# PEER row gathers spread over the second stage, and DeltaNet head norms begun at the scans' ends, in a one-core diffusion layer

## Chip, cores and metric

One core of one Trainium2 chip runs the whole layer in one launch. The metric is device time in microseconds; lower is better. The times of the kernel before are three runs: 2075.72, 2077.7 and 2087.32 us, median 2077.7 us.

## What is computed

A layer over 512 latent tokens (D = 1024) with 256 context tokens ahead of them, then a final norm; all in fp32. Cut to what matters here:

```python
m = project_mixer_inputs(h, w_in, ...)            # q, k, v of attention and DeltaNet, z, gates
o_attn = windowed_attention(...)
o_dn, _, _ = bidirectional_delta(m, ..., st_f, st_b)   # 4 heads of 128, scans in both directions
o_dn = gated_head_norm(o_dn, m['z_dn'], dn_norm)  # o * rsqrt(mean(o*o, -1) + eps) * gain * silu(z), per token and head
x = x + gt1 * (m['gate_attn'] * (o_attn @ w_br_attn) + m['gate_dn'] * (o_dn @ w_br_dn)) @ w_out
h2 = rmsnorm(x, norm_ffn) * (1.0 + sc2) + sh2
x = x + gt2 * peer_ffn(h2, ...)                   # 8 heads x top 16 of 128*128 experts for each token:
                                                  # sum of gate * gelu(h2 . u_table[e]) * v_table[e]
return rmsnorm(x, final_norm)
```

## The kernel before

TensorE multiplies in pairs of high and low halves: each fp32 operand is split into a rounded high part (a cast on ScalarE) and the rest (a subtraction on GpSimd or VectorE), and `mm3` (lines 173 to 176) issues three products for each.

**DeltaNet** (up to 632 us). `dn_front`, `dn_batch` and `dn_scan(h)` are generators that a loop (lines 1032 to 1053) steps in turn, at a raised priority; the build's scheduler then orders the instructions of each engine by priority and by when it reckons them ready. The scans of the four heads overlap in part. `dn_scan` makes six steps; a step's state update goes TensorE, ScalarE (`vt`, line 936, a tile with two buffers that all scans share), TensorE, VectorE. From the third step on it writes the token outputs `od[:, l, h]` (lines 963 to 966), each from both directions.

**Merge** (lines 1202 to 1253). All sixteen pairs of token block `l` and head `h` get a square with a sum on ScalarE (line 1206), into `oss`; one scaling, one square root, one reciprocal and one multiplication of all of `od` follow (lines 1208 to 1211). Then head by head: a gate tile is loaded (`gate_tile`, line 1199, three buffers), TensorE transposes the head (1216), VectorE multiplies by gate and gain (1217), and ScalarE and VectorE split the result into `dT` (1218, 1219). The products with w_br_dn follow (lines 1238 to 1253). The rows gt1b, sh2b, a2b and the norm's gain are loaded after that in the program (1257 to 1261), and VectorE scales gt1b and makes a2b (1260, 1262). `out_proj` (line 1274) multiplies by w_out in eight chunks for a pair of token blocks and then uses gt1b (1295) and a2b (1303).

**PEER** takes two ways. For three of the four token blocks (ND = 3) all 128 blocks of 128 experts are computed densely: `first_product` multiplies u by the tokens, a gelu follows, then the weighting by a gate matrix (from DRAM, `gg`) and `second_product` with v, accumulated in PSUM. In the first stage `nb` = 112 blocks get their first product, and the activations go to DRAM (`Ad`); the second stage computes the other 16, and makes the second product of all 128. The fourth token block (LG) gathers: each of 128 (head, choice) rows of u, then of v, is read for all 128 tokens by one indirect DMA on GpSimd's queue into one of four `grow` buffers (lines 1439, 1450); VectorE makes a dot product of each u row (1432) and adds each v row to `accg` (1454).

The gathers run as a side task, `gu = Side(chain(gather_u(), gather_v()))`: `run(us)` adds credit, and the generator goes on as long as credit is left; a row costs 1.2 (0.3 for the first three). GpSimd's and VectorE's order is the program's own here. In the second stage's loop, slot `n` computes block `ORDER[n]` (the 16 new ones first), prepares the operands of block `n - 5` (`operands`, lines 1533 to 1553: loads of v, gates and stored activations on the SP queue, weighting on VectorE, casts on ScalarE), gives the gathers credit, and issues the second product of the block before. In the credit, `first` is true for slots 5 to 15:

```python
            first, put_by = b >= nb and n < NBLK, ORDER[n - SKEW] < nb
            gu.run(GF * (4.18 - 1.25 - 1.1 + (4.16 - 2.5) * first))
            if not fin and (gu.done or n == NBLK + SKEW - LAST - 1):
                gu.run(1e9)
                finish(LG)
```

`finish(LG)` (lines 1574 to 1601) adds the residual and applies the final norm for the gathered block. `second_product` subtracts for the low halves (1556, 1557) and holds the last four blocks (LAST = 4) back, to run them as one group by token block. The three dense blocks are finished after it.

Of the kernel before, what the change touches and what calls it, by code (L numbers as in the profile page):

```python
# [62 lines left out]
MWAIT = 3  # L63
SKEW = 5
OT = 4
GF = 1.0
GWAIT = 2
TKG = 3.6
GU = 0.8
# [67 lines left out]
def body(ctx: ExitStack, tc: tile.TileContext, I, out, dbg=lambda *a: None):  # L137
# [5 lines left out]
    def const(shape, name, dt=F32):  # L143
        return cp.tile(shape, dt, name=name, tag=name)
# [768 lines left out]

    scanned = set()

    def dn_scan(h):

        unit = heads[h]["unit"]
# [2 lines left out]
        for step in range(6):  # L921
# [48 lines left out]
                dbg(f"S{h}", Sn)  # L970
            yield
        scanned.add((h, 6))

# [52 lines left out]
    live, scans, nscan = [], [], 0  # L1028
    side = [beside()]
    tick = 0  # L1030
    oss = const([P, NLB, 4], "oss")
    while front or live or batches or scans or nscan < 4:
        with tc.high_priority(offset=FIRST):
            with tc.high_priority(offset=FRONT):
# [165 lines left out]
        return t  # L1200


    for l in range(NLB):
        for h in range(4):
            junk = gst([P, P], "junkn", bufs=2)
            S.activation(junk, od[:, l, h], AF.Square, accum_out=oss[:, l, h:h + 1])
    dbg("od", od)
    V.tensor_scalar(oss, oss, 1.0 / P, EPS, op0=ALU.mult, op1=ALU.add)
    S.activation(oss, oss, AF.Sqrt)
    V.reciprocal(oss, oss)  # L1210
    V.tensor_tensor(od, od, oss[:, :, :, None].to_broadcast([P, NLB, 4, P]), op=ALU.mult)
    for h in range(4):
        szh = gate_tile(16 + h)
        pt = psum()
# [42 lines left out]
    SP.dma_start(gt1b, bc(arows[0], P, D))  # L1257
    SP.dma_start(sh2b, bc(arows[1], P, D))
    SP.dma_start(a2b, bc(arows[2], P, D))
    V.tensor_scalar(gt1b, gt1b, 0.5, None, op0=ALU.mult)  # L1260
    SP.dma_start(nfb, bc(I["norm_ffn"][0], P, D))
    V.scalar_tensor_tensor(a2b, a2b, 1.0, nfb, op0=ALU.add, op1=ALU.mult)

    qp = mg.tile([P, HEADS, SEQ], F32, name="qp", tag="dT")
    h2T_hi = mp.tile([P, KC, SEQ], F32R, name="h2T_hi", tag="oT")
# [8 lines left out]
    def out_proj(pair):  # L1274
# [5 lines left out]
        for k in range(KC):  # L1280
            raw = raw_tile()
            SP.dma_start(raw, I["w_out"][0, k * P:(k + 1) * P])
            hi, lo = split(raw)
            for l in pair:
                ls = slice(l * P, (l + 1) * P)
                for j in range(2):
                    js = slice(j * 512, (j + 1) * 512)
                    mm3(acc[l, j], yT_hi[:, k, ls], yT_lo[:, k, ls], hi[:, js], lo[:, js], k == 0, k == KC - 1)
# [110 lines left out]
    def gate_matrices(l):  # L1399
# [5 lines left out]
        for t0 in range(0, P, TB):  # L1405
# [21 lines left out]
            for i0 in range(0, KEYS, 32):  # L1427
                S.dma_start(Gd[pc, :, i0:i0 + 32], stg[:, i0:i0 + 32])

    def gather_u():  # L1430
        def dot(j, u):
            V.tensor_tensor_reduce(out=u, in0=u, in1=h2p if stage[0] < 2 else h2g, scale=1.0, scalar=0.0, op0=ALU.mult, op1=ALU.add,  # L1432
                                   accum_out=act[:, j:j + 1])
            return 1.2

        held = []
        for j in range(P):
            u = gp.tile([P, D], F32, name="grow", tag="grow", bufs=4)
            G.indirect_dma_start(out=u, out_offset=None, in_=UT_, in_offset=bass.IndirectOffsetOnAxis(ap=exi[:, j:j + 1], axis=0))  # L1439
            held.append((j, u))  # L1440
            yield dot(*held.pop(0)) if len(held) > DOTLAG else 0.3
        for x in held:
            yield dot(*x)
        S.activation(act, act, AF.Gelu_apprx_tanh)
        V.tensor_tensor(act, act, gateg, op=ALU.mult)

    def gather_v():
        for j in range(P):
# [3 lines left out]
                V.tensor_scalar(accg, v, act[:, 0:1], None, op0=ALU.mult)  # L1452
            else:
                V.scalar_tensor_tensor(accg, v, act[:, j:j + 1], accg, op0=ALU.mult, op1=ALU.add)  # L1454
            yield 1.2

    def transpose_u(b):

# [144 lines left out]
    for n in range(NBLK + SKEW):  # L1603
# [12 lines left out]
                ws[n] = w  # L1616
        if n >= SKEW:
            nxt.append(operands(n - SKEW, ws.pop(n - SKEW, None)))
            first, put_by = b >= nb and n < NBLK, ORDER[n - SKEW] < nb
            gu.run(GF * (4.18 - 1.25 - 1.1 + (4.16 - 2.5) * first))  # L1620
            if not fin and (gu.done or n == NBLK + SKEW - LAST - 1):
                gu.run(1e9)
                finish(LG)
            if len(nxt) > 1:
                second_product(*nxt.pop(0))
# [43 lines left out]
```

## Time and profile before

| | before |
|---|---|
| median of 3 runs | 2077.7 us (2075.72 to 2087.32) |
| profiled execution, its own time | 2080.87 us |
| its span | 2079.1 us |
| mean granted TensorE clock | 0.969 |
| TensorE (PE) | 1928.9 us busy, 93% |
| VectorE (DVE) | 1643.1 us, 79% |
| ScalarE (ACT) | 951.1 us, 46% |
| GpSimd (POOL) | 976.9 us, 47% |
| HBM traffic | 228 GB/s over the span |

The profiled execution is one run on its own; its time is 3.2 us above the median. Busy shares are averages over all stages. A busy TensorE is pipelined, and the ends of its matmuls are modelled. The row "idle before" or the bracket behind an instruction names what ended the idle time of its engine.

### The profile page before, as it was taken

The numbers are of one execution on the slowest core, as the hardware profiler recorded it, in microseconds if no ns is written. First come the engines' busy times: TensorE is split into PE (matmuls) and PEld (weight loads), VectorE is DVE, ScalarE is ACT, GpSimd is POOL, SyncE is SP. The second block draws the span as 40 slices with busy tenths as digits, with TensorE's granted clock in tenths as the row PEclk, the third lists the DMA queues.
The fourth block names the chain that finished last, engine by engine and source line by source line (L and its number), as shares of the span: only waits on it lengthen the run. The fifth ranks groups of instructions, "written<-read, shape, count | busy, mean of one in ns | idle before, by whom it ended". The sixth has DMA issues, their size and how long they took to land.

```text
span 2079.1 us, 29606 instructions
## 1 busy us (share of the span) xinstructions
PE 1928.9 (93%) x10018; PEld 1627.8 (78%) x10018; DVE 1643.1 (79%) x3304; ACT 951.1 (46%) x1769; POOL 976.9 (47%) x695
## 2 busy tenths in 40 slices
PE   6999999999897897999999999899889999999998
PEld 2766666788786696989999999888778777777786
DVE  4599885378776768799998999666879898989855
ACT  5545544333333443333766666895323333333333
POOL 2655534311212872677565666443445555555200
PEclk9999999999998998999999999999999999999999
DMA  9333322422515685889889878789999999999963
GB/s 308 92 112 116 107 82 81 127 84 63 138 51 182 201 195 158 234 234 252 242 255 266 246 236 256 242 259 309 300 315 376 386 386 393 389 391 397 352 233 107
DMA packets 283477, 475.87 MB, mean 229 GB/s; under 512 B 35224, under 2 KB 197293, under 8 KB 282813
## 3 DMA queue, kind: packets, MB, share of 16 engines
q1 hardware_dynamic: 214251, 277.82, 43.9%
q0 software_dynamic: 36864, 134.23, 18.9%
q10 hardware_dynamic: 32210, 61.93, 8.4%
q8 instruction: 79, 1.29, 0.3%
q14 instruction: 73, 0.60, 0.1%
HBM read 409.71 MB, written 64.18 MB: 228 GB/s over the span
## 4 chain that ended last, share of the span: by engine, by line
PE 36%; DMA 17%; DVE 14%; issue 14%; POOL 12%; ACT 5%; ACTq 1%; SPq 1%; DVEq 0%; POOLq 0%
DMA grow<-in_peer_v_dram,exi 7%; POOL w_lo L1470 7%; POOL grow L1439 3%; PE pg L176 3%; PE pg L175 3%; PE pg L174 3%; PE pacc L175 3%; PE pacc L176 2%; PE pacc L174 2%; PE pa L176 2%; PE pa L174 2%; PE pa L175 2%; DMA rep<-ad 2%; DVE accg L1454 2%; PE pm L1422 2%
## 5 line engine op out<-in xcount | busy, mean ns | idle before, releaser
L1470 POOL TENSOR_TENSOR w_lo<-ut,w_hi 128x512 fp32r<-128x512 f32 x224 | 293.9, 1335 | 231.4 <-ACT w_hi L1466 225.3
L174 PE MATMUL pa<-h2T_hi,w_hi 128*128 128x384 f32 x1024 | 354.6, 346 | 35.2 <-ACT w_hi L1466 32.4
L176 PE MATMUL pa<-h2T_hi,w_lo 128*128 128x384 f32 x1024 | 361.2, 354 | 9.3 <-POOL w_lo L1470 8.4
L175 PE MATMUL pa<-h2T_lo,w_hi 128*128 128x384 f32 x1024 | 349.9, 342 | 0.0
L170 POOL TENSOR_TENSOR w_lo<-w_raw,w_hi 128x1024 fp32r<-128x1024 f32 x78 | 200.1, 2576 | 305.1 <-ACT w_hi L169 229.3
L1450 POOL DMA_INDIRECT grow<-in_peer_v_dram,exi x128 | 200.0, 1563 | 168.0 <-DVE accg L1454 143.4
L1552 ACT CAST w_hi<-w_raw 128x1024 fp32r<-128x1024 f32 x124 | 130.3, 1051 | 226.3 <-DMA w_raw<-in_peer_v_dram 110.8
L175 PE MATMUL pacc<-w_lo,wh 128*128 128x512 f32 x744 | 214.0, 403 | 20.1 <-DVE w_lo L1556 19.5
L174 PEld LDWEIGHTS pa<-h2T_hi,w_hi 128*128 128x128 f32 x1024 | 198.3, 194 | 43.3 <-ACT w_hi L1466 42.8
L176 PEld LDWEIGHTS pa<-h2T_hi,w_lo 128*128 128x128 f32 x1024 | 197.8, 193 | 16.0 <-POOL w_lo L1470 13.1
L176 PE MATMUL pacc<-w_hi,wl 128*128 128x512 f32 x744 | 208.8, 396 | 0.0
L174 PE MATMUL pacc<-w_hi,wh 128*128 128x512 f32 x744 | 208.3, 395 | 0.0
L175 PEld LDWEIGHTS pa<-h2T_lo,w_hi 128*128 128x128 f32 x1024 | 197.5, 193 | 0.3
L1439 POOL DMA_INDIRECT grow<-in_peer_u_dram,exi x128 | 148.3, 1159 | 100.4 <-DVE act L1432 80.4
L175 PEld LDWEIGHTS pacc<-w_lo,wh 128*128 128x128 f32 x744 | 138.6, 190 | 63.0 <-DVE w_lo L1556 31.7
L1466 ACT CAST w_hi<-ut 128x1024 fp32r<-128x1024 f32 x126 | 132.6, 1053 | 114.6 <-DVE ut L1465 80.4
L1454 DVE SCALAR_TENSOR_TENSOR accg<-grow,act,accg 128x1024 f32<-128x1024 f32 x127 | 162.8, 1282 | 25.1 <-DMA grow<-in_peer_v_dram,exi 24.1
L1556 DVE TENSOR_TENSOR w_lo<-w_raw,w_hi 128x1024 fp32r<-128x1024 f32 x124 | 151.3, 1220 | 33.7 <-ACT w_hi L1552 33.7
L176 PEld LDWEIGHTS pacc<-w_hi,wl 128*128 128x128 f32 x744 | 140.6, 189 | 34.3
L174 PEld LDWEIGHTS pacc<-w_hi,wh 128*128 128x128 f32 x744 | 139.4, 188 | 34.7 <-ACT wh L1543 0.5
L1465 DVE STREAM_TRANSPOSE ut<-w_raw 128x1024 f32<-128x1024 f32 x126 | 155.8, 1238 | 10.7 <-DMA w_raw<-in_peer_u_dram 7.9
L174 PE MATMUL pg<-hL_hi,w_hi 128*128 128x512 f32 (+1 forms) x336 | 139.6, 416 | 0.0
(447 smaller groups left out, 4115.9 us busy)
## 6 DMA issues: line engine op xcount, KB each, us to landing
w_raw<-in_peer_u_dram SPq DMA_DIRECT2D x512, 128.0 KB
w_raw<-in_peer_v_dram SPq DMA_DIRECT2D x128, 512.0 KB
Gd<-stg ACTq DMA_DIRECT2D x48, 512.0 KB
gg<-Gd SPq DMA_DIRECT2D x16, 1536.0 KB
Ad<-ga ACTq DMA_DIRECT2D x112, 192.0 KB
aa<-Ad SPq DMA_DIRECT2D x28, 768.0 KB
w_raw<-in_w_ada_dram SPq DMA_DIRECT2D x40, 512.0 KB
w_raw<-in_w_in_dram SPq DMA_DIRECT2D x34, 512.0 KB
```

Source lines behind the costliest of these rows:

```text
L170: (lo_eng or G).tensor_tensor(lo, raw, hi.bitcast(F32), op=ALU.subtract)
L174: PE.matmul(o, lh, rh, start=start, stop=False)
L175: PE.matmul(o, lh, rl, start=False, stop=False)
L176: PE.matmul(o, ll, rh, start=False, stop=stop)
L1439: G.indirect_dma_start(out=u, out_offset=None, in_=UT_, in_offset=bass.IndirectOffsetOnAxis(ap=exi[:, j:j + 1], axis=0))
L1450: G.indirect_dma_start(out=v, out_offset=None, in_=VT_, in_offset=bass.IndirectOffsetOnAxis(ap=exi[:, j:j + 1], axis=0))
L1454: V.scalar_tensor_tensor(accg, v, act[:, j:j + 1], accg, op0=ALU.mult, op1=ALU.add)
L1465: V.transpose(lf.rearrange("p (c f q) -> p c f q", f=4, q=32), u.rearrange("p f (c x) -> p c f x", x=32))
L1466: S.copy(hi, lf)
L1470: eng.tensor_tensor(lo[:, cs], lf[:, cs], hi[:, cs].bitcast(F32), op=ALU.subtract)
L1552: S.copy(vh, v)
L1556: V.tensor_tensor(vl, v, vh.bitcast(F32), op=ALU.subtract)
```

## The change

At the end of the scans of heads 0, 1 and 2 the squares of the head's four token blocks and the scaling of their sums are issued (`head_norm`); `oss` is laid out by head and made before the scans. In the merge the three heads get square root, reciprocal and a multiplication of their own each, then head 3 its squares and the rest. The two VectorE instructions on gt1b and a2b are issued in `out_proj`, at the fifth chunk of w_out of the first pair. In PEER's second stage the credit of a slot is the rows still to do, times 1.3, shared over the slots up to 127, where a slot that computes a new block counts twice; a v row costs 1.3 instead of 1.2.

```diff
+    oss = const([P, 4, NLB], "oss")
+    def head_norm(h):
+        junk = dn.tile([P, 2, P], F32, name="vt", tag="vt", bufs=2)
+        for l in range(NLB):
+            S.activation(junk[:, l % 2], od[:, l, h], AF.Square, accum_out=oss[:, h, l:l + 1])
+        V.tensor_scalar(oss[:, h], oss[:, h], 1.0 / P, EPS, op0=ALU.mult, op1=ALU.add)
...
         scanned.add((h, 6))
+        if h < 3:
+            head_norm(h)
...
+    def scale_heads(hs):
+        S.activation(oss[:, hs], oss[:, hs], AF.Sqrt)
+        V.reciprocal(oss[:, hs], oss[:, hs])
+        for h in range(4)[hs]:
+            V.tensor_tensor(od[:, :, h], od[:, :, h], oss[:, h, :, None].to_broadcast([P, NLB, P]), op=ALU.mult)
+    scale_heads(slice(0, 3))
     for l in range(NLB):
-        for h in range(4):
-            junk = gst([P, P], "junkn", bufs=2)
-            S.activation(junk, od[:, l, h], AF.Square, accum_out=oss[:, l, h:h + 1])
-    V.tensor_scalar(oss, oss, 1.0 / P, EPS, op0=ALU.mult, op1=ALU.add)
-    S.activation(oss, oss, AF.Sqrt)
-    V.reciprocal(oss, oss)
-    V.tensor_tensor(od, od, oss[:, :, :, None].to_broadcast([P, NLB, 4, P]), op=ALU.mult)
+        junk = gst([P, P], "junkn", bufs=2)
+        S.activation(junk, od[:, l, 3], AF.Square, accum_out=oss[:, 3, l:l + 1])
+    V.tensor_scalar(oss[:, 3], oss[:, 3], 1.0 / P, EPS, op0=ALU.mult, op1=ALU.add)
+    scale_heads(slice(3, 4))
...
     SP.dma_start(a2b, bc(arows[2], P, D))
-    V.tensor_scalar(gt1b, gt1b, 0.5, None, op0=ALU.mult)
     SP.dma_start(nfb, bc(I["norm_ffn"][0], P, D))
-    V.scalar_tensor_tensor(a2b, a2b, 1.0, nfb, op0=ALU.add, op1=ALU.mult)
+    def rows_ready():
+        V.tensor_scalar(gt1b, gt1b, 0.5, None, op0=ALU.mult)
+        V.scalar_tensor_tensor(a2b, a2b, 1.0, nfb, op0=ALU.add, op1=ALU.mult)
...
             hi, lo = split(raw)
+            if pair == PAIRS[0] and k == 4:
+                rows_ready()
...
+    rows = [2 * P]
     def gather_u():
         def dot(j, u):
+            rows[0] -= 1
...
-            yield 1.2
+            rows[0] -= 1
+            yield 1.3
...
-            first, put_by = b >= nb and n < NBLK, ORDER[n - SKEW] < nb
-            gu.run(GF * (4.18 - 1.25 - 1.1 + (4.16 - 2.5) * first))
+            part = [1 + (m < NBLK and ORDER[m] >= nb) for m in range(n, NBLK + SKEW - LAST - 1)]
+            if part:
+                gu.run(1.3 * rows[0] * part[0] / sum(part))
```

## Rows read from the trace of the kernel before

**Rows 1.** Busy time by stretch: stretch, length, engines (instructions), clock, DMA share, GB/s.
```profile
400.00:613.00 213.00, 195.59 (x1253) 174.15 (x1251) 163.08 (x567) 70.54 (x144) 42.28 (x20) 0.94 0.32 88
631.00:647.00 16.00, 4.70 (x25) 4.54 (x24) 7.71 (x13) 7.51 (x36) 1.80 (x1) 0.59 0.76 279
1450.00:1550.00 100.00, 86.76 (x398) 74.34 (x396) 77.98 (x110) 30.46 (x40) 45.19 (x31) 0.95 1.00 310
1660.00:1960.00 300.00, 292.10 (x1230) 228.91 (x1229) 272.54 (x311) 104.49 (x138) 157.26 (x101) 1.00 1.02 392
1980.00:2052.00 72.00, 72.00 (x310) 57.94 (x309) 39.75 (x56) 27.10 (x36) 0.00 (x0) 1.00 0.60 202
...
1840.00:1860.00 20.00, 19.54 (x84) 15.76 (x85) 19.30 (x23) 7.62 (x10) 10.52 (x9) 1.00 1.00 372
```

**Rows 2.** Waits by waiter and releaser in the merge: us in total, times, longest.
```profile
PE pt L1216 <- DVE ods L1211: 11.3, 1, 11.3
...
DVE h2t L1295 <- PE pt L176: 8.6, 1, 8.6
```

**Rows 3.** Order of time at the merge's head: start, length, engine, line, operation.
```profile
632.57 0.35 DVE L966 SCALAR_TENSOR_TENSOR ods<-pt,rq,ods 128x128 f32<-128x128 f32 x1
...
636.93 1.28 ACT L1209 ACT_TABLE_LOAD   x1
...
638.48 0.25 DVE L1210 RECIPROCAL oss<-oss 128x16 f32<-128x16 f32 x1 [1.35 <-ACT oss L1209]
639.76 0.69 DVE L1260 TENSOR_SCALAR gt1b<-gt1b 128x1024 f32<-128x1024 f32 x1 [1.03 <-DMA gt1b<-arows]
640.37 2.28 DVE L1211 TENSOR_TENSOR ods<-ods,oss 128x2048 f32<-128x2048 f32 x1
...
647.64 0.71 PE L174 MATMUL pt<-dT,w_hi 128*128 128x512 f32 x2
...
631.57 1.28 SPq L1199 DMA_DIRECT2D gA<-gates  x3
```

**Rows 4.** Order of time on ScalarE in the last scans.
```profile
586.78 0.60 ACT L860 ACTIVATE at<-pt 128x512 f32<-128x512 f32 x1 [1.66 <-PE pt L771]
...
622.64 0.63 ACT L936 ACTIVATE vt<-pt,etail 128x128 f32<-128x128 f32 x2 [3.18 <-PE pt L932]
626.45 0.68 ACT L936 ACTIVATE vt<-pt,etail 128x128 f32<-128x128 f32 x2 [3.18 <-PE pt L932]
```

**Rows 5.** Order of time on VectorE: a block's low half (line 1556), one a slot.
```profile
1554.80 1.22 DVE L1556 TENSOR_TENSOR w_lo<-w_raw,w_hi 128x1024 fp32r<-128x1024 f32 x1
...
1950.68 1.22 DVE L1556 TENSOR_TENSOR w_lo<-w_raw,w_hi 128x1024 fp32r<-128x1024 f32 x1
...
1955.27 1.22 DVE L1556 TENSOR_TENSOR w_lo<-w_raw,w_hi 128x1024 fp32r<-128x1024 f32 x1
...
1958.54 1.22 DVE L1556 TENSOR_TENSOR w_lo<-w_raw,w_hi 128x1024 fp32r<-128x1024 f32 x1
...
2020.60 1.22 DVE L1556 TENSOR_TENSOR w_lo<-w_raw,w_hi 128x1024 fp32r<-128x1024 f32 x1 [2.04 <-ACT w_hi L1552]
...
2041.60 1.22 DVE L1556 TENSOR_TENSOR w_lo<-w_raw,w_hi 128x1024 fp32r<-128x1024 f32 x1 [2.04 <-ACT w_hi L1552]
```

**Rows 6.** VectorE's waits from 1580 to 1960 us.
```profile
DVE accg L1454 <- DMA grow<-in_peer_v_dram,exi: 24.1, 26, 2.0
```

**Rows 7.** Order of time at the end of the gathered token block.
```profile
1960.61 0.68 DVE L1591 TENSOR_TENSOR of<-accg,gt2b 128x512 f32<-128x512 f32 x1
...
1967.25 1.22 DVE L1556 TENSOR_TENSOR w_lo<-w_raw,w_hi 128x1024 fp32r<-128x1024 f32 x1
...
1968.52 2.93 PE L175 MATMUL pacc<-w_lo,wh 128*128 128x512 f32 x6 [2.75 <-DVE w_lo L1556]
```

**Rows 8.** Groups by line from 1340 us on: count, busy, mean ns, idle before.
```profile
L1432 DVE CUSTOM_DVE_ANT_0 grow<-grow,h2g 128x1024 f32<-128x1024 f32 x47 | 55.9, 1219 | 8.1 <-DMA grow<-in_peer_u_dram,exi 8.1
...
L1596 ACT ACT_TABLE_LOAD x1 | 1.3, 1283 | 0.0
```

More of the change, by code (lines that the diff above doesn't have):

```diff
@@ L65 @@
 OT = 4
-GF = 1.0
 GWAIT = 2
@@ L1030, in body @@
     tick = 0
-    oss = const([P, NLB, 4], "oss")
     while front or live or batches or scans or nscan < 4:
@@ L1200, in gate_tile @@
         return t
-    for l in range(NLB):
-        for h in range(4):
-            junk = gst([P, P], "junkn", bufs=2)
-            S.activation(junk, od[:, l, h], AF.Square, accum_out=oss[:, l, h:h + 1])
-    dbg("od", od)
-    V.tensor_scalar(oss, oss, 1.0 / P, EPS, op0=ALU.mult, op1=ALU.add)
-    S.activation(oss, oss, AF.Sqrt)
-    V.reciprocal(oss, oss)
-    V.tensor_tensor(od, od, oss[:, :, :, None].to_broadcast([P, NLB, 4, P]), op=ALU.mult)
+    def scale_heads(hs):
[4 more added lines that the diff above has]
+    scale_heads(slice(0, 3))
+    for l in range(NLB):
+        junk = gst([P, P], "junkn", bufs=2)
+        S.activation(junk, od[:, l, 3], AF.Square, accum_out=oss[:, 3, l:l + 1])
+    V.tensor_scalar(oss[:, 3], oss[:, 3], 1.0 / P, EPS, op0=ALU.mult, op1=ALU.add)
+    scale_heads(slice(3, 4))
     for h in range(4):
```

## Prediction

> **What bounds the kernel now.** The page gives TensorE 93% of the span, an average, so I read the busy time stretch by stretch [rows 1] and stopped wherever TensorE was not full next to code that the change touches. There are three such places.
>
> The first is the head of the merge. From 631 to 647 us TensorE is busy for 4.70 of 16 us, and the waits name one cause: the transposes of line 1216 sat 11.3 us until the multiplication of line 1211 was done [rows 1, 2]. The order of time [rows 3] shows what fills those 11.3 us: the last DeltaNet output at 632.57, sixteen squares on ScalarE up to 636.9, a table load of 1.28 us, the square root, the reciprocal at 638.48, then 1.03 us in which VectorE stands before the scaling of gt1b until its DMA has landed, that scaling, and the multiplication of all heads, 2.28 us long. The first product of the merge begins at 647.64.
>
> The second is the gate-weighted part of PEER's second stage, after the sixteen blocks that are computed there. From 1660 to 1960 us the DMA share is 1.02 at 392 GB/s, and TensorE loses 7.9 us of 300; from 1980, when no row is gathered any more, TensorE is busy for 72.00 of 72 us with the DMA at 0.60 [rows 1]. A block shows once on VectorE, as the subtraction that makes its low half. From 1554.80 to 1958.54 there are 94 of these, so 403.74 us over 93 slots, 4.34 us each; from 2020.60 to 2041.60 five slots take 21.00 us, 4.20 each [rows 5]. So 4.20 is TensorE's own pace, and the gathering costs 93 x 0.14 = 13.1 us. VectorE sees it as 24.1 us of waiting for gathered rows [rows 6].
>
> The third is the end of the gathered token block: VectorE spends 1960.61 to 1967.25 on it, and the next block's products wait 2.75 us [rows 7].
>
> **The change part by part.** I sum against the profiled execution's own 2080.87 us (span 2079.1 and 1.8 around it), which lies 3.2 above the median of 2077.7; the differences are then taken from the median.
>
> *Rows spread evenly.* 47 of the 128 dots of u fall in the second stage [rows 8], so 47 + 128 = 175 rows are left at its start. Walked by the code, the old rule (3.49 us of credit in each of the first 11 slots, 1.83 in the others, 1.2 a row) gives 32 rows to the first 11 slots and then 1.525 a slot, and is done near slot 110, where the rows show the end [rows 7]. The new rule (weight 2 for the first 11, 1 for 112 more) gives 31 and then 144 / 112 = 1.286 a slot, to the last.
> Bytes of a slot, from the shapes: 512 KiB of v, 192 of gates, 192 of stored activations, 512 a row. Before: 1677 KiB, 1.717 MB, in 4.34 us: 395 GB/s, what the DMA row says too. After: 1554 KiB, 1.592 MB, in 4.20 us: 379 GB/s, 4% under that rate. VectorE: a slot with one row runs in 3.27 us (1955.27 to 1958.54), one with two in 4.59 (1950.68 to 1955.27) [rows 5], so 3.65 on average, under 4.20. Both fit, TensorE is the bound, and of 13.1 us I let 2.1 remain as jitter, for 4% is little: **-11** (bounds: -13.1 if all goes; -4.2 if the DMA gives only 372 GB/s, the lowest 20 us slice there [rows 1]).
> The first 11 slots are VectorE's and the DMA's (1.00 share at 310 GB/s [rows 1]); one dot fewer at 1.2 us: **-1** (0 to -3).
>
> *The Trainium skill against it.* The row comes first: 392 GB/s over 300 us, one core running [rows 1]. The Trainium skill, page "DMA: Bandwidth & Descriptors", section "Where 436 GB/s comes from", holds that between HBM and SBUF the HBM side, about 358 GB/s for a core, is what binds; by it a slot would take an estimated 1.592 / 0.358 = 4.45 us, this term would be 112 x 0.25 - 13.1 = +14 instead of -11, and the whole would land near 2084. The trace disagrees: it moves more than that for 300 us.
>
> *The end of the gathered block moves* from about slot 110 to slot 128, five before the end. With it go its VectorE chain (6.64 us), two squares, a square root and its table load on ScalarE, and on the SP queue a load of the final gain and two stores, now behind some 18 more loads of v. The wait of 2.75 us moves along and is no new cost. What can be new: after it VectorE owes six blocks at 2.1 us each. The last four run as one group, and its fourth block is wanted 2 x 4.20 + 3 x 1.4 = 12.6 us after the products resume; VectorE can have it after 5 x 2.1 = 10.5 (2.1 is its work in a slot without a row, 3.27 less 1.2). So little: **+0.5** (bounds -1, when it falls into a wider lead, to +5, when the 6.64 us are hidden by nothing).
>
> *Merge.* Twelve squares leave the stretch; three heads' norms need only tensors that exist already, so they can run from the end of the third scan on, in the gaps of the fourth. For head 3 remain, from 632.9: one square after its last output (0.3, and 0.2 to read the sum), 0.2 scaling, 0.2 root, 0.25 reciprocal, about 0.7 for a 512-wide multiplication: 634.8 instead of 642.65. The table load is no longer in that chain. gt1b's scaling and a2b leave VectorE's queue there (1.03 us of waiting, 0.6 and 1.2 us of work) and go beside w_out's fifth chunk, where VectorE next waits 8.6 us for the pair's last product [rows 2]; both are wanted only after the last product of the pair, so nothing, and if VectorE were full there, 1.8. What is late next is the gate tiles: SP issues them at 631.57 [rows 3], 0.79 MB at the 279 GB/s of that stretch, so 634.4. Then product with the gate 0.75, cast 0.6, subtraction 0.7: the first product near 636.5 instead of 647.64. That is 11 us; the fourth head's gate has to wait for a buffer and the order on TensorE is fixed beforehand, so I take **-9.5** (bounds -12 and -4). What follows hangs on these products and moves along.
> *The second square root.* Square roots of three heads, then squares, then one more root. In the end of the kernel four roots with squares between them need one table load [rows 8], so no load is added. The Trainium skill, "ScalarE: Activation LUTs", section "Table sets: the hidden batching unit", wants functions batched by set at about 2.7 us a switch; were the square outside the root's set, that would be an estimated 5 us more here; the trace shows it is not.
>
> *Scans.* Each of three scans gets four squares (0.3 us each) and a scaling of 0.2 us at high priority. ScalarE is busy for 70.5 of 213 us there, TensorE for 196 [rows 1]; but ScalarE takes its work in order, and behind a square that waits for its output stand other heads' evacuations. Least nothing, most one scan step (622.64 to 626.45, 3.8 us [rows 4]) three times, 11 us; with ScalarE two thirds idle I stay near nothing: **+1.5**. The early root's table load falls where only copies run, since the last exponential is at 586.78 [rows 4].
>
> Sum: -11 - 1 + 0.5 - 9.5 + 1.5 = -19.5. From 2077.7: **2058**.
>
> **The rivals.**
> *The transfers stay the bound.* For it: the share of 1.02 and only 4% of room; row reads wait for four buffers. Against: what is moved on average is 4% more than the new slot needs, and loads run some slots ahead. At 372 GB/s 112 slots take 178.3 MB / 0.372 = 479 us, 9 over TensorE's 470: -13.1 + 9 - 8.5 (the other terms) = -12.6, **2065**.
> *The merge only exchanges its wait*: the change does not do what it says, because the heads' multiplications stay behind the fourth scan (their output tile is shared with it), or the gates come late. For it: SP's first gate issue waits for the fourth scan's buffers. Against: each head has slices of its own. Merge -4: **2063**.
> *Slower: a lower DMA rate with gathers in every slot.* The first 11 slots move 310 GB/s at a full share; gate pieces and gathers now run to the end, where 19 slots had none. At 351 GB/s, halfway between 310 and 392, the 112 slots take 508 us, 38 over TensorE's: +38 - 13.1 - 8.5 = +16, **2094**. It decides below 355 GB/s. Against: that low rate goes with loads of u in 1 KB pieces, which do not occur later.
> The Trainium skill's 358 GB/s, named above, is this mechanism at another price: an estimated 498 us for the 112 slots and 2084 in all; no row here shows it.
>
> **How the numbers follow.** 0.70 for the forecast, 0.12 transfers stay the bound, 0.11 for the merge's wait, 0.07 for the lower rate, most of it below 355 GB/s. The range goes from 2048 (merge -12, gathering -13.1, first slots -3, tail -1: -29) to 2070, past the first two rivals with some cost in the scans or the tail. About 0.5% (10.4 us) is what a measurement of this kernel can tell from no change. Faster by more: nearly all of the forecast and three quarters of the first two rivals, 0.66 + 0.17 = 0.83; slower: 0.05 of the last; within: the rest, 0.12.
>
> **What would show it.** In the changed profile: the wait of line 1216 down from 11.3 us to under 3, and the first merge product some 10 us earlier relative to the fourth scan's end; slots of 4.20 to 4.23 us and a DMA share under 1 from 1550 on; gathers until the last slots; the wait of some 3 us within the last 30 us. It is wrong if slots stay at 4.3 us or more with a full DMA share, if the stage from 400 to 632 us grows by over 5 us, or if TensorE waits before the last four blocks.

## Result and the profile after

The changed kernel takes **2058.73 us** (median of 4 runs, 2055.5 to 2065.32) against 2080.76 (4 runs of the kernel before, 2075.72 to 2087.32): ratio 0.9896, 95% interval 0.9856 to 0.9936. The forecast was 2058 in 2048 to 2070. Its profiled execution took 2055.5 us with a span of 2053.7; the span before was 2079.1.

To see where 25.4 us of span went I cut every profile at five points that both kernels have: ScalarE's last tanh of the projections (before's line 983), the start of the last DeltaNet output (line 966), the first h2t product of the merge (line 1295), the first w_lo of the second stage (line 1556), and the end. Worked out from the first and last starts of these lines in each trace, in us:

| profile | to the tanh | scans | merge | merge to stage 2 | stage 2 |
|---|---|---|---|---|---|
| before | 360.6 | 272.0 | 65.5 | 766.4 | 614.6 |
| after | 355.4 | 274.9 | 58.6 | 764.4 | 600.4 |
| spread alone | 355.6 | 271.8 | 63.5 | 771.3 | 596.1 |
| merge alone | 356.9 | 274.6 | 58.6 | 770.2 | 620.2 |
| after, second profile | 359.7 | 275.0 | 61.7 | 771.6 | 605.0 |
| weight 1.5 | 354.6 | 274.8 | 61.2 | 768.6 | 598.3 |
| weight 1.5, second profile | 354.6 | 275.0 | 61.3 | 768.1 | 593.6 |
| weight 1 | 359.1 | 272.3 | 58.8 | 760.3 | 597.9 |
| half rows (in before) | 359.1 | 271.6 | 64.4 | 768.3 | 610.5 |
| extra load | 355.8 | 273.4 | 58.6 | 774.1 | 720.2 |
| head 3's squares in vt | 360.6 | 273.6 | 62.1 | 770.6 | 604.5 |
| head 3's squares in mid | 360.2 | 275.7 | 61.1 | 768.3 | 603.4 |
| head 3 late on TensorE | 355.6 | 272.7 | 63.6 | 765.2 | 601.1 |
| the same with weight 1.5 | 356.0 | 274.1 | 61.5 | 762.8 | 598.2 |

The rows from the third on are the experiments below. The first and the fourth column hold the same work in every row and still differ by 6 and 14 us. A difference of 5 us in one pair of profiles therefore shows nothing by itself; of the 25.4 us, 5.2 lie ahead of anything that the change touches. What repeats: against the row of before, stage 2 is 10 to 19 us shorter wherever after's spread stands (but for the extra load), the merge 4 to 7 us wherever its part stands as in after, and the scans are 0.3 to 3.0 us longer there.

The stretches after, columns as in [rows 1]:

```profile
400.00:608.00 208.00, 187.92 (x1216) 167.96 (x1214) 152.13 (x529) 73.55 (x159) 41.20 (x20) 0.93 0.31 86
629.00:645.00 16.00, 8.99 (x43) 7.65 (x42) 10.99 (x20) 3.24 (x12) 1.80 (x1) 0.79 0.91 332
1450.00:1550.00 100.00, 88.96 (x407) 76.31 (x406) 79.88 (x113) 31.43 (x42) 44.65 (x31) 0.96 0.96 297
1660.00:1960.00 300.00, 300.00 (x1287) 241.38 (x1286) 264.55 (x309) 107.99 (x144) 149.84 (x93) 1.00 1.00 384
```

The last row is the result: from 1660 to 1960 us TensorE is busy for 300.00 of 300 us, where it was busy for 292.10 [rows 1]. The DMA share is still 1.00, at 384 GB/s, but TensorE no longer waits for what the transfers bring. The second row is the merge's head, 8.99 of 16 us where it was 4.70.

VectorE's wait for gathered rows from 1580 to 1960 us (as [rows 6]), and its order of time around the end of the gathered block (as [rows 7]):

```profile
DVE accg L1474 <- DMA grow<-in_peer_v_dram,exi: 2.2, 4, 1.2
```
```profile
2002.68 1.23 DVE L1577 TENSOR_TENSOR w_lo<-w_raw,w_hi 128x1024 fp32r<-128x1024 f32 x1 [0.46 <-ACT w_hi L1573]
...
2006.81 0.69 DVE L1613 TENSOR_TENSOR of<-of,xl 128x512 f32<-128x512 f32 x1
2012.87 0.16 DVE L1615 TENSOR_TENSOR rs<-rs 128x1 f32<-128x1 f32 x1 [5.37 <-ACT sq L1614]
...
2015.91 1.22 DVE L1577 TENSOR_TENSOR w_lo<-w_raw,w_hi 128x1024 fp32r<-128x1024 f32 x1
```

Waiting for gathered rows fell from 24.1 us [rows 6] to 2.2. The end of the gathered block cost VectorE 6.64 us before (1960.61 to 1967.25 [rows 7]); now it is 11.15, from 2004.76 to 2015.91. ScalarE's order of time there, and TensorE's next row:

```profile
2010.00 1.05 ACT L1573 CAST w_hi<-w_raw 128x1024 fp32r<-128x1024 f32 x1 [3.15 <-PE pacc L175]
...
2011.36 0.63 ACT L1614 ACTIVATE sq<-of 128x512 f32<-128x512 f32 x1
```
```profile
2017.19 1.66 PE L174 MATMUL pacc<-w_lo,wh 128*128 128x512 f32 x6 [1.67 <-DVE w_lo L1577]
```

On ScalarE the cast of the next block stands ahead of the two squares and waits 3.15 us for TensorE to free its buffer; VectorE waits 5.37 us for the squares. Before had the same order, but there VectorE had no lead, so the buffer came free sooner, and the cast began ahead of the block's end:

```profile
1960.25 1.05 ACT L1552 CAST w_hi<-w_raw 128x1024 fp32r<-128x1024 f32 x1 [2.27 <-PE pacc L176]
```

TensorE feels 1.67 us of it, less than the 2.75 before [rows 7], since VectorE came here with more blocks in hand. The 2.75 us also cost more than themselves: from 1968.50 to 1973.00 the granted clock was 0.63 of full speed in before, and the six products behind the wait took 2.93 us [rows 7]; after the 1.67 us it stayed at 1.00, and six took 1.66.

### The profile page after: what moved, and what is told of

Read it like the earlier page. It is cut to its first block, busy times and chain, and to the rows that moved or that the text cites. A ratio compares the mean times of both kernels' runs of the same rounds, so it can differ in the third digit from the quotient of the medians.

```text
span 2053.7 us, 29600 instructions
## 1 busy us (share of the span) xinstructions
PE 1912.8 (93%) x10018; PEld 1622.3 (79%) x10018; DVE 1637.4 (80%) x3311; ACT 951.4 (46%) x1770; POOL 978.9 (48%) x695
## 4 chain that ended last, share of the span: by engine, by line
PE 37%; POOL 9%; DMA 6%; issue 6%; ACT 6%; DVE 4%; ACTq 1%; SPq 1%; DVEq 0%; POOLq 0%
PE pacc L174 8%; PE pacc L175 8%; PE pacc L173 8%; POOL w_lo L1491 6%; PE pa L175 3%; PE pa L173 3%; PE pa L174 3%; DMA w_raw<-in_peer_u_dram 3%; ACT o L1433 2%; ACT stg L1440 2%; PE pm L1439 2%; POOL grow L1459 2%; POOL w_lo L169 1%; ACT w_hi L1487 1%; DMA w_raw<-in_peer_wq_dram 1%
## 5 line engine op out<-in xcount | busy, mean ns | idle before, releaser
L1470 POOL DMA_INDIRECT grow<-in_peer_v_dram,exi x128 | 205.0, 1601 | 211.6 <-DVE accg L1474 190.1
L174 PE MATMUL pacc<-w_lo,wh 128*128 128x512 f32 x744 | 194.6, 396 | 9.2 <-DVE w_lo L1577 9.2
L175 PE MATMUL pacc<-w_hi,wl 128*128 128x512 f32 x744 | 193.7, 395 | 0.0
L173 PE MATMUL pacc<-w_hi,wh 128*128 128x512 f32 x744 | 193.7, 395 | 0.0
```

Source lines behind the costliest of these rows:

```text
L173: PE.matmul(o, lh, rh, start=start, stop=False)
L174: PE.matmul(o, lh, rl, start=False, stop=False)
L175: PE.matmul(o, ll, rh, start=False, stop=stop)
L1470: G.indirect_dma_start(out=v, out_offset=None, in_=VT_, in_offset=bass.IndirectOffsetOnAxis(ap=exi[:, j:j + 1], axis=0))
```

## The experiments

### The two parts alone

"Spread alone" has the new credit rule in the kernel before; "merge alone" is the changed kernel with the old rule:

```diff
-            part = [1 + (m < NBLK and ORDER[m] >= nb) for m in range(n, NBLK + SKEW - LAST - 1)]
-            if part:
-                gu.run(1.3 * rows[0] * part[0] / sum(part))
+            gu.run(1.0 * (4.18 - 1.25 - 1.1 + (4.16 - 2.5) * first))
```

> Only the rows' credit in PEER's second stage is changed, the merge is the one before. Theory (the second stage pays by itself): blocks at 4.20 us instead of 4.34 from the seventeenth on, TensorE without a gap until the gathered block's end, and 10 to 15 us less in all, ratio 0.993 to 0.995. Rival (the profiled pair's difference in this stage, 14 us, is partly the state of that run): under 8 us. Rival (a wait takes the place of the one removed): the end of the gathered block costs more than the 2.75 us it did, and the gain is under 8 us.

> Only the merge and the scans are changed, the rows' credit is the one before. Theory: the first merge product comes some 5 us earlier after the fourth scan than before, the scans cost up to 3 us, what follows keeps it: 4 to 8 us less in all, ratio 0.996 to 0.998. Rival (what the profiled pair differs by before the first scan ends, where both kernels issue the same instructions, is most of it): no difference, ratio 0.999 to 1.001.

Measured, on one chip where the kernel before took 2083.54 (17 runs): spread alone 2062.81 (6 runs), ratio 0.9903 [0.9874, 0.9931]; merge alone 2080.02 (12 runs), ratio 0.9968 [0.9946, 0.999]. TensorE's waits from 1550 to 1990 us, in before and in merge alone:

```profile
PE pacc L175 <- DVE w_lo L1556: 13.5, 12, 3.5
```
```profile
PE pacc L174 <- DVE w_lo L1577: 15.8, 13, 4.8
```

In spread alone this view has no row at all, and the stretch from 1660 to 1960 reads:

```profile
1660.00:1960.00 300.00, 300.00 (x1287) 241.35 (x1286) 264.86 (x310) 107.56 (x144) 140.56 (x93) 1.00 1.01 384
```

The window of these waits does not hold the same in every kernel. Of before's 13.5 us, 3.48 end the first slots (at 1551.71) and 2.75 the gathered block (at 1968.52 [rows 7]). Both are still there with the spread, outside the window: 3.1 us at 1548.6 and 1.7 at 2025.1 in spread alone. The 7.3 us between them, in ten waits, are gone. The stage cut at the 11th w_lo (#10) and at the 120th (#119) shows where, in us:

| profile | #0 to #10 | #10 to #119 | #119 to the end |
|---|---|---|---|
| before | 90.3 | 470.0 | 54.3 |
| merge alone | 94.2 | 471.7 | 54.2 |
| spread alone | 88.3 | 451.7 | 56.1 |
| after | 89.3 | 451.7 | 59.4 |

109 slots at TensorE's own 4.20 us [rows 5] are 457.8 us. With the spread the rows on VectorE come in 6.1 less: VectorE runs ahead of TensorE, so its rows do not give the slot's cost. TensorE's own rows do: the start of its products with the low half of block #10 and of block #103, the last one ahead of the gathered block's end in before. In before, then in after:

```profile
1557.58 1.56 PE L175 MATMUL pacc<-w_lo,wh 128*128 128x512 f32 x6
...
1961.40 1.56 PE L175 MATMUL pacc<-w_lo,wh 128*128 128x512 f32 x6
```
```profile
1544.95 1.56 PE L174 MATMUL pacc<-w_lo,wh 128*128 128x512 f32 x6
...
1935.55 1.56 PE L174 MATMUL pacc<-w_lo,wh 128*128 128x512 f32 x6
```

The same cut in every profile, from TensorE's first product of the stage with a block of v on, in us:

| profile | to #10 | #10 to #103 | #103 to the end |
|---|---|---|---|
| before | 105.4 | 403.8 | 117.7 |
| merge alone | 109.3 | 403.8 | 119.4 |
| half rows (in before) | 111.3 | 390.6 | 120.6 |
| spread alone | 102.3 | 390.6 | 114.9 |
| the five others with weight 2, as in after | 103.4 to 108.6 | 390.6 | 117.9 to 118.2 |
| weight 1.5, three profiles | 93.3 to 94.8 | 391.5 to 396.4 | 117.9 to 118.5 |
| weight 1 | 87.7 | 392.7 | 123.7 |

93 slots at 4.20 us are 390.6. All six profiles with weight 2 have it to the tenth, and before and merge alone have 13.2 us more: the spread takes away the whole of the gathering's cost.

The last column holds something that no part alone shows. In the kernels with both parts the program ends 12.2 to 12.5 us behind TensorE's last product, in before, merge alone and spread alone 9.2 to 9.4. VectorE begins the end of the first dense token block later against TensorE's last product (which ends at 2049.16 in spread alone, at 2041.26 in after); spread alone, then after:

```profile
2037.99 0.69 DVE L1595 TENSOR_TENSOR of<-pacc,gt2b 128x512 f32<-128x512 f32 x1 [2.05 <-PE pacc L176]
```
```profile
2033.12 0.69 DVE L1612 TENSOR_TENSOR of<-pacc,gt2b 128x512 f32<-128x512 f32 x1 [4.55 <-PE pacc L175]
```

The scheduler sets TensorE's order in the last group: in spread alone it keeps the token blocks nearly apart, in after it mixes the first with the others, so its sums are complete 3 us later. No run changed that order by itself; about 3 us may be left there.

The merge part's third piece, `rows_ready`, moves nothing. With that edit alone the program has the instructions of before in the same order on all five engines, and after still scales gt1b at 637.69 and forms a2b at 642.67 (rows below).

### Half the bytes of a gathered row, in the kernel before

Left out: the second half of each v row; the first half is used twice, so VectorE's work stays and a row brings half the bytes.

```diff
-            G.indirect_dma_start(out=v, out_offset=None, in_=VT_, in_offset=bass.IndirectOffsetOnAxis(ap=exi[:, j:j + 1], axis=0))
+            G.indirect_dma_start(out=v[:, :512], out_offset=None, in_=VT_.rearrange("e (a f) -> (e a) f", f=512), in_offset=bass.IndirectOffsetOnAxis(ap=exi[:, j:j + 1], axis=0))
+            vv = v[:, None, :512].to_broadcast([P, 2, 512])
...
-                V.scalar_tensor_tensor(accg, v, act[:, j:j + 1], accg, op0=ALU.mult, op1=ALU.add)
+                V.scalar_tensor_tensor(av, vv, act[:, j:j + 1], av, op0=ALU.mult, op1=ALU.add)
```

> The kernel before with its own credit of rows, but each v row is read by half, 512 of 1024 columns (256 KB an issue), and the half is used twice on VectorE, so that VectorE and GpSimd issue as before; the second half of the expert sums of one token block is left out. Theory (bytes bound the slots): a slot asks for 1.32 MB, 314 GB/s at 4.20 us, and slots run at 4.20 us with TensorE full. Rival (the number of rows, VectorE's order or GpSimd's issue bounds them): slots stay at 4.3 us or more.

Measured: 2075.63 us (one run). Slots #35 to #103 took 4.194 us (before: 4.355). The stretch from 1660 to 1960, and VectorE's wait for rows from 1580 to 1960:

```profile
1660.00:1960.00 300.00, 297.62 (x1276) 239.10 (x1274) 275.28 (x318) 106.43 (x147) 142.54 (x101) 1.00 0.87 304
```
```profile
DVE accg L1456 <- DMA grow<-in_peer_v_dram,exi: 0.3, 1, 0.3
```

With the burst and its number of rows kept and only bytes taken away, the share falls to 0.87, VectorE's wait for rows to 0.3 us, and the slot to TensorE's 4.20; on TensorE's rows #10 to #103 takes 390.6 us, as with the spread (table above). It is one run, and in whole only 8 us under before, since its first slots and its end are longer. The old 4.34 us was a matter of bytes in the slot, as the prediction had it, not of the number of rows or of VectorE's work on them.

### More bytes in a slot, in the changed kernel

```diff
         SP.dma_start(v, VT_[b * P:(b + 1) * P])
+        if b < nb:
+            SP.dma_start(pkt([32, D], "pad", bufs=1), VT_[b * P:b * P + 32])
```

> The changed kernel with one more load of 128 KB (rows of v, used by nothing) in each slot of a stored block, some 117 of them, 1.72 MB a slot in place of 1.59. The theory by bytes: at 392 GB/s a slot takes 4.39 us in place of 4.13, and where the transfers' real limit is 405 to 415, 4.15 to 4.25 us: with 4.39 the kernel is 20 to 28 us longer, TensorE waits for w_lo in most slots, as in the kernel before. Rival: the transfers have room left and only the burst of the kernel before cost its time: under 4 us more, 4.13 to 4.17 us a slot.

Measured: 2183.89 us (one run), which fits neither. The stretch from 1660 to 1960, SP's waits from 1600 to 2000, and the end:

```profile
1660.00:1960.00 300.00, 287.56 (x1203) 228.09 (x1203) 242.68 (x284) 98.89 (x132) 153.13 (x86) 0.98 1.02 364
```
```profile
SPq L1562 <- DMA pad<-in_peer_v_dram: 80.0, 18, 9.1
```
```profile
2123.00 56.34 SPq L1562 DMA_DIRECT2D pad<-in_peer_v_dram  x26
```

I gave the load one buffer, so each waits on SP for the one before, with the loads of v behind it: 80.0 us in that window. Some 9 loads per 100 us were issued where about 23 had been meant, and the last 26 run alone at the end, 2.17 us each. About 55 us of the time are those 26. TensorE's loss of 12.4 of 300 us goes with that queue of loads and shows nothing of how much room a slot has; the rate at which the room ends stays open.

### Where in stage 2 the rows go

Weight 1.5 and weight 1 in place of 2 for the first 11 slots. Counted in the traces, they get 24 and 17 rows in place of 31, so 2.2 and 1.5 in each in place of 2.8, somewhat more than the expectations below say:

```diff
-            part = [1 + (m < NBLK and ORDER[m] >= nb) for m in range(n, NBLK + SKEW - LAST - 1)]
+            part = [1 + 0.5 * (m < NBLK and ORDER[m] >= nb) for m in range(n, NBLK + SKEW - LAST - 1)]
```

> The changed kernel once more, on the chip that timed its parts. Theory: the two parts lie in different stages and add up; stage 2 alone gave about 20.7 us (2062.8 of 2083.5) and the merge and the scans alone 3.5 us in the median, where its milestones gave 4.2 (merge -6.9, scans +2.7); so 2058 to 2060 and a ratio of 0.988. Rival: the parts do not add, since both wait for the same end of stage 2; then 2062 to 2063, as with the spread alone.

> The first 11 slots of stage 2 get half more rows than the others (about 2.04 each, 1.36 in the others) and not twice as many (2.58 and 1.29). Theory that the first 11 slots are bound by VectorE and GpSimd (88 us for ten slots in the profile of the spread alone, 8.8 us a slot) and the later ones by TensorE: each row less takes up to 1.2 to 1.3 us from a first slot, 0.55 rows times 11 slots is 7 us at most, and the later slots ask for 1.63 MB in 4.14 us, 393 GB/s, which the transfers just carry: 2 to 6 us under the changed kernel. Rival: the first slots are bound by something else, or the later slots are at the transfers' limit already: no change, or 1 to 4 us more, with 4.15 to 4.20 us a slot and TensorE waiting for w_lo.

> Every slot of stage 2 weighs the same: 1.42 rows in each, where the first 11 had 2.58 in the changed kernel and 2.04 with weight 1.5. Theory: the first slots lose their last VectorE wait with weight 1.5 already (TensorE's wait for w_lo there fell from 7.5 to 0.7 us), so little is left to gain at the front (0 to 5 us), and the others ask for 1.66 MB, 4.22 to 4.24 us at 392 GB/s in place of 4.16, which gives back 5 to 9 us over 112 slots: 0 to 6 us over the time of weight 1.5 (2051), TensorE waiting for w_lo more often. Rival (the transfers have room): another 3 to 6 us under weight 1.5.

> The kernel with weight 1.5 a second time, since its 2050.8 us and the 2056.3 of weight 1 lie within the spread of single runs (2048 to 2063). Theory: the front's VectorE wait is gone for good (TensorE's wait for w_lo before 1550 us under 1.5 us again, the first ten slots 80 to 83 us), and the time is 2048 to 2054, a ratio of 0.982 to 0.986. Rival: 2051 was a lucky draw and the later slots give the gain back: 2055 to 2060, a ratio of 0.987 to 0.990, like the changed kernel's.

Measured (the first two rows side by side on one chip, the others each in a session of its own):

| kernel | median us (runs) | ratio to before, 95% | #0 to #10 | #10 to #119 | #119 to the end |
|---|---|---|---|---|---|
| after, again | 2057.24 (5) | 0.987 [0.9851, 0.989] | 92.3 | 453.2 | 59.5 |
| weight 1.5 | 2050.83 (5) | 0.9842 [0.9825, 0.986] | 81.5 | 458.9 | 57.9 |
| weight 1 | 2056.31 (6) | 0.9886 [0.986, 0.9913] | 77.8 | 460.3 | 59.9 |
| weight 1.5, again | 2053.69 (6) | 0.9865 [0.9838, 0.9892] | 81.1 | 458.1 | 54.4 |

TensorE's wait for w_lo from 1420 to 1550 us, after and then weight 1.5:

```profile
PE pacc L174 <- DVE w_lo L1577: 7.5, 7, 2.2
```
```profile
PE pacc L174 <- DVE w_lo L1577: 0.7, 2, 0.5
```

The first slots hung on VectorE's queue, where the gathered rows' dot products stand ahead of the block's low half. With fewer rows VectorE's rows there take 8 to 14 us less, and TensorE reaches #10 after 93.3 to 94.8 us, with weight 1 after 87.7, where weight 2 takes 102.3 to 108.6 (table on TensorE's rows above). Fewer rows are also fewer bytes, and no run separates the two there. Some of it is given back: #10 to #103 takes TensorE 391.5 to 396.4 us, and 392.7, where weight 2 has 390.6. In the first profile of weight 1.5 all 5.8 us of that are one place, a wait of 2.77 us at 1751.99, behind a load of stored activations that VectorE waits 2.72 us for, and slow products after it (six in 2.93 us). The whole stage is 593.6 to 598.3 us with the lower weights, 596.1 to 605.0 with weight 2. Weight 1 gains 4 us more at the front than weight 1.5 and loses them in the other two columns. Weight 1.5 has the two lowest medians of all, 6.4 and 3.6 us under after's 2057.24, but its intervals overlap after's: both beat the kernel before, and that weight 1.5 also beats after is likely, not settled by these runs. (The last experiment below has the two weights once more in one session, with head 3 late in both: 2055.98 against 2066.06, and there the intervals lie apart.) After's parts do add up (0.9903 and 0.9968 make 0.987).

### The fourth head's wait: its squares

Squares of head 3 at its scan's end too, first into the scan's own tile `vt`, then (second diff) into a part of `mid` that nothing else uses by then:

```diff
-        if h < 3:
-            head_norm(h)
+        head_norm(h)
...
-        junk = dn.tile([P, 2, P], F32, name="vt", tag="vt", bufs=2)
+        junk = dn.tile([P, 2, P], F32, name="vt", tag="vt", bufs=2) if h < 3 else mid[:, 0, :2 * P].rearrange("p (a f) -> p a f", f=P)
```

> The changed kernel, and the squares of the fourth head too are issued at its scan's end, into the scans' own buffer. Theory (head 3's norm is late because its squares wait for the merge's memory and so fall behind the other heads' gate products on VectorE): its multiplication ends some 4 us earlier after the scan than in the changed kernel, the first merge product comes 3 to 4 us earlier, and the whole is 3 to 4 us under the changed kernel. Rival (the gate tiles' transfers are next): at most 1 us.

> The fourth head's squares also at its scan's end, now into memory that no load of the merge waits for, so the gates' loads start as early as in the changed kernel. Theory: the wait of TensorE for the fourth head (5.4 us) was set by the squares' wait for memory that the scans still held (the first square is 6 us late to its place) and by what stands ahead of the head's multiplication on VectorE; without the first, the first product comes 1 to 4 us earlier after the last write of od, and the time is 1 to 4 us under the changed kernel. Rival: the chain after it (gates, gate products of the other heads, the casts) sets the merge's start all the same: within 1 us.

Measured: 2069.49 (6 runs), ratio 0.9924 [0.9895, 0.9952], and 2066.78 (6 runs), ratio 0.9913 [0.9888, 0.9939]. To see why, first after's own merge head, in order of time on VectorE, ScalarE, TensorE and SP:

```profile
630.31 0.35 DVE L974 SCALAR_TENSOR_TENSOR ods<-pt,rq,ods 128x128 f32<-128x128 f32 x1
632.00 1.41 DVE L1230 SCALAR_TENSOR_TENSOR gA<-pt,hnorm,gA 128x512 f32<-128x512 f32 x2 [1.34 <-PE pt L1229]
633.33 0.16 DVE L1223 TENSOR_SCALAR oss<-oss 128x4 f32<-128x4 f32 x1
634.48 0.75 DVE L1230 SCALAR_TENSOR_TENSOR gA<-pt,hnorm,gA 128x512 f32<-128x512 f32 x1 [0.99 <-DMA gA<-gates]
635.15 1.28 DVE L1232 TENSOR_TENSOR dT<-gA,dT 128x512 fp32r<-128x512 f32 x2
636.35 0.17 DVE L1214 RECIPROCAL oss<-oss 128x4 f32<-128x4 f32 x1
636.44 0.66 DVE L1232 TENSOR_TENSOR dT<-gA,dT 128x512 fp32r<-128x512 f32 x1
637.01 0.68 DVE L1216 TENSOR_TENSOR ods<-ods,oss 128x512 f32<-128x512 f32 x1
637.69 0.69 DVE L1276 TENSOR_SCALAR gt1b<-gt1b 128x1024 f32<-128x1024 f32 x1
...
642.67 1.23 DVE L1277 SCALAR_TENSOR_TENSOR a2b<-a2b,nfb 128x1024 f32<-128x1024 f32 x1
```
```profile
631.99 0.19 ACT L1222 ACTIVATION_READ_ACCUMULATOR junkn<-ods 128x1 f32 x1
632.79 1.28 ACT L1231 CAST dT<-gA 128x512 fp32r<-128x512 f32 x2 [0.61 <-DVE gA L1230]
633.97 0.20 ACT L1213 ACTIVATE oss<-oss 128x4 f32<-128x4 f32 x1
```
```profile
637.75 1.12 PE L1229 MATMUL pt<-cst,ods 128*128 128x128 f32 x4 [5.44 <-DVE ods L1216]
638.66 1.91 PE L1246 MATMUL pt<-cst,w_raw 128*128 128x128 f32 x8
640.23 0.78 PE L173 MATMUL pt<-dT,w_hi 128*128 128x512 f32 x1
```
```profile
629.31 1.27 SPq L1208 DMA_DIRECT2D gA<-gates  x3
```

The squares are over at 632.18, but the norm needs four more small steps, and each stands behind the other heads' work: the scaling behind two gate products, the root behind two casts, the reciprocal behind a third gate product (itself 0.99 us late by its DMA) and two subtractions, the multiplication behind one more subtraction. From the end of the last output (630.66) to the end of L1216 (637.69) it is 7.03 us. In the second variant it is 6.96 (636.23 to 643.19), and TensorE's wait, from the view of waits, is the same:

```profile
PE pt L1224 <- DVE ods L1215: 5.4, 1, 5.4
```

The squares' place is thus not what sets this wait. The first variant shows the other side: the gates' tiles lie where `vt` lay, so SP waits 2.3 us for the squares and issues them 0.9 us after the last output's end (634.56), where after has them 1.35 ahead of it, and VectorE waits for them. With nothing else to do it runs the norm at once, and L1216's counterpart ends 2.25 us after the last output, close to the prediction's 1.9; but TensorE then waits for the gate products instead: its first product comes 5.1 us after the last output, as hoped, but it runs without gaps only from 9.2 us on, and the merge is 62.1 us. VectorE's and SP's order of time, and VectorE's wait from 630 to 660:

```profile
636.12 0.69 DVE L1215 TENSOR_TENSOR ods<-ods,oss 128x512 f32<-128x512 f32 x1
```
```profile
635.46 1.27 SPq L1207 DMA_DIRECT2D gA<-gates  x3
```
```profile
DVE gA L1225 <- DMA gA<-gates: 5.9, 2, 4.4
```

Why the second variant's median lies 9.5 us over after's on the same chip is open: its profile shows no stage that is clearly longer (scans 275.7, merge 61.1, stage 2 603.4), but after's profile of that session is its slowest run by far (2074.73 us) and no yardstick.

### The fourth head's wait: its place on TensorE

```diff
-    for h in range(4):
+    for h in range(3):
+        head_out(h)
...
             for c in range(4):
+                if m == 0 and c == 3:
+                    head_out(3)
                 mm3(pB, hi[:, c, fs], lo[:, c, fs], dT_hi[:, c], dT_lo[:, c], c == 0, c == 3)
```

"Best" is this with weight 1.5.

> In the changed kernel the fourth head's transposes stand ahead of everything else on TensorE in the merge (5.4 us of waiting, first product 9.6 us after the last write of od), though the first product's terms of three heads need nothing of the fourth. Here the fourth head is transposed only ahead of its own term of the first product, and the keys' transposes come before. Theory (the order on TensorE is what is left of the wait): the first product comes 5 to 6.5 us after the last write of od, a shorter wait for head four's gate product (1 to 3 us) is left behind the first terms, and the merge ends 2 to 5 us earlier: a time of 2052 to 2056, against 2057 to 2059. Rival (VectorE's queue sets the start, since the casts of keys and gate products stand in the same order there): the first product is no earlier than 9 us after it, and the time stays within 1 us.

> Both at once: first slots at weight 1.5, and the fourth head's transposes behind the other heads' terms. Theory: they lie in different stages and add up, 2046 to 2050, a ratio near 0.982, the shortest of all. Rival: the earlier merge is lost again in PEER's first stage, whose length differs by several us from run to run: 2050 to 2053.

Measured: 2066.06 (9 runs), ratio 0.9941 [0.9918, 0.9963]; best 2055.98 (6 runs), ratio 0.9882 [0.9863, 0.9902]. The theories missed: the time is not shorter than after's, and "best" is no better than weight 1.5 alone. Whether it is longer is not settled: the interval lies apart from after's second one (0.9851 to 0.989) and overlaps its first (0.9856 to 0.9936). The merge of the table is 63.6 and 61.5 us in the two profiles, against 58.6 to 61.7 with after's. TensorE, VectorE and SP at its head in the first, in order of time, where the last output ends at 628.66:

```profile
631.50 0.49 PE L173 MATMUL pt<-dT,w_hi 128*128 128x512 f32 x1 [0.32 <-ACT dT L1231]
635.61 0.79 PE L174 MATMUL pt<-dT,w_hi 128*128 128x512 f32 x1 [3.61 <-DVE dT L1232]
```
```profile
633.45 0.67 DVE L1251 COPY keysT<-pt 64x512 f32<-64x512 f32 x1
...
645.29 0.75 DVE L1230 SCALAR_TENSOR_TENSOR gA<-pt,hnorm,gA 128x512 f32<-128x512 f32 x1 [3.85 <-DMA gA<-gates]
```
```profile
635.58 12.18 SPq L1208 DMA_DIRECT2D gA<-gates  x4
```

TensorE does start sooner, with one matmul at 2.8 us and the rest from 6.95 us after the last output (after: 9.57). But VectorE now copies keys ahead of the subtraction that the second matmul needs, and the fourth head's gate takes its turn in a ring of three tiles behind gates of the later products: its DMA is 3.85 us late at 645.29. What was won at the head is lost behind it: 36 to 39 us after the last output TensorE waits 2.3 us for the sum of a later product, in both profiles, which it does not in after's. By the table the merge ends 2 to 5 us later than after's in the first profile and within after's range in the second; any further distance to after is open.

## Why the prediction was right

The total was right to a microsecond, and that is luck. The mechanism of the largest term held, but the terms' sizes were off, and two errors of some 4.5 us cancel (the second stage gave more, the merge less). The base moved too: the forecast was -19.5 us from 2077.7, and measured were -22.0 from 2080.76.

- **Spread, -11 (bounds -13.1 to -4.2).** Measured on TensorE's rows: -13.2, from 403.8 to 390.6 us over #10 to #103, the same in all six profiles with weight 2. The cost of 13.1 us was read rightly, and that bytes set it was shown by the half rows. The step at fault is "of 13.1 us I let 2.1 remain as jitter": nothing remained, at 384 GB/s with 1.592 MB a slot. Stage 2 over these six profiles (596.1, 600.4, 605.0, and 604.5, 603.4, 601.1 in the three kernels with head 3 moved) has a mean of 601.8, against 617.4 for before and merge alone: -15.6 (-16.0 by TensorE's rows), where the sum over this stage said -11.5. About half of the difference is this term; the first slots and the tail are the rest.
- **First 11 slots, -1 (0 to -3).** On TensorE's rows a mean of 107.3 us to #10 without the spread and of 105.6 with it, -1.8: sign and size hold, though the single profiles overlap. The larger lever was there and not in my list: weight 1.5 takes 12 us more from them (93.9) and gives some 4 back behind them.
- **Tail, +0.5 (-1 to +5).** VectorE's chain grew from 6.64 to 11.15 us, since the cast ahead of the squares now waits for TensorE: a lead of VectorE means a later free buffer, which I had not priced. TensorE paid 1.67 us in place of 2.75, because the lead covered it, and kept its clock; the last group of four showed no wait. "The wait of 2.75 us moves along and is no new cost" left out that it got cheaper: from #103 to the end spread alone takes 114.9 us, where before and merge alone have a mean of 118.6. With both parts it is 117.9 to 118.2, for the order of the last group gives 3 us back. So the net of -1.0 is near the forecast by luck.
- **Merge, -9.5 (-12 to -4).** Measured: -5.15 from the last output to the first product (14.72 to 9.57), and a mean of 59.8 us for seven profiles with after's merge, against 64.5 for three without: -4.6, near the weak end. The first number is the firmer one: in all seven profiles the first product comes 9.5 to 9.9 us after the last output, in the three without 14.7 to 14.8. Two steps failed. "For head 3 remain ... 634.8 instead of 642.65" added bare durations, 1.9 us, where VectorE and ScalarE work in order and the other heads' products, casts and subtractions stand between: 7.03 us. The 2.25 us of the variant with late gates shows that the durations were right and the order was missing. And gt1b and a2b were to "leave VectorE's queue there": the edit moves the place in the code, the build's scheduler put them where they had been. The wait of 11.3 us [rows 2] came to 5.4, not under 3. The rival "the merge only exchanges its wait" was half true; its price, -4, was the better number.
- **Scans, +1.5 (0 to 11).** Nine profiles with the squares have a mean of 274.1 us, three without 271.8: +2.3, near the forecast. The trace shows one way to it: squares of head 2 lie between the two activations that feed a scan step and hold the second up by some 0.3 us. Where the rest arises is not shown.

```profile
609.72 0.37 ACT L944 ACTIVATE vt<-pt,etail 128x128 f32<-128x128 f32 x1 [4.86 <-PE pt L938]
609.98 0.30 ACT L921 ACTIVATE vt<-ods 128x128 f32<-128x128 f32 x1
...
610.27 0.35 ACT L944 ACTIVATE vt<-pt,etail 128x128 f32<-128x128 f32 x1
...
611.66 1.28 ACT L1213 ACT_TABLE_LOAD   x1
```

- **The table load** fell in the scans, as said, and no second one came with the fourth head's root at 633.97. The Trainium skill, "ScalarE: Activation LUTs", section "Table sets: the hidden batching unit", gives about 2.7 us for a load; the one here takes 1.28, and the root follows right behind it, at 612.95.
- **The rivals from the transfers** fell. They needed a rate under what the spread asks for; the transfers carried 384 GB/s for 300 us and TensorE had no gap. The 358 GB/s of the Trainium skill, "DMA: Bandwidth & Descriptors", section "Where 436 GB/s comes from", is again passed; by it the kernel would have been slower.

Summed from the profiles: -15.6 - 4.6 + 2.3 = -17.9, against -22.0 by the medians and within the timed interval (-0.64% to -1.44%, or -13 to -30 us).

## What to carry to other kernels

Where two bounds are close (here bytes of a slot and TensorE's 4.20 us), spreading a side task so that no slot exceeds the second bound can take away the whole wait, as it did here with 4% of room; then ask which slots are bound by a third engine and give them less. A chain of short steps costs what stands ahead of each step on its in-order engine, not the sum of its durations: read the order around it before pricing it. A cost is read from the rows of the engine that is the bound: VectorE's rows mixed the slot's cost with a lead that it built or lost. Moving a line of code is no move of an instruction where a scheduler sets the order.

## What the runs showed that I had not expected

- Stages with the same instructions differ by 6 us (to the last tanh) and 14 us (760.3 to 774.1, the stretch between merge and stage 2) from profile to profile; only a table over several kernels separates terms of 2 to 5 us.
- VectorE's rows of a block can run faster than TensorE (4.14 us a slot against 4.20) for a hundred slots: that pace is a lead being built, not the slot's cost.
- Loads of 128 KB into one buffer, one after another on SP, take 2.17 us each with nothing else running (26 in 56.34 us).
- Two changes in different stages still met: with both in, the scheduler orders TensorE's last group otherwise, and the end of the program is some 3 us longer than with the spread alone.
